# The attention branch's projection by one level of Strassen's method

## The chip, the cores and the metric

One Trainium2 chip, of which the kernel uses one core. The metric is the device time of one execution in microseconds. The kernel before takes 1419.27 us, the median of three runs (1418.53 to 1420.07). The engines are called PE (matrix multiply), ACT (activations, casts, copies), DVE (elementwise work), POOL, and SP, whose queue issues nearly every DMA.

## What is computed

One layer of an encoder on 1024 tokens of 1024 channels, in float32. The part that matters here is the end of the token mixer: two branches, attention `y_a` and recurrence `y_b`, each of 512 channels, are projected to 1024 channels, weighed by sigmoid gates, added, and projected once more.

```
p_a = y_a @ w_pa                      # (1024, 512) @ (512, 1024)
p_b = y_b @ w_pb
merged = sigmoid(gate_a) * p_a + sigmoid(gate_b) * p_b
mix = merged @ w_o
x = layer_norm(ALPHA * x + mix, ln1_g, ln1_b)
x = layer_norm(ALPHA * x + swiglu_ffn(x, w_ff_in, w_ff_out), ln2_g, ln2_b)
```

## The kernel before

**Precision.** PE multiplies in a rounded form of float32. Each operand is split into a high part (a cast on ACT) and a low part (a subtraction on DVE; `split`, line 444), and each product of two 128-row blocks is three matmuls: high by high, high by low, low by high (`mm3`, line 473). A matmul here takes a 128 x 128 weight block and 512 tokens, and accumulates in one of eight PSUM banks.

**Order of the work.** The program text does not run as written. `Plan` records every instruction with what it depends on; a list scheduler with a table of costs (`schedule`, line 183, repeated by `improve`, line 355) then sets one fixed order for each engine, and `issue` (line 387) emits it. So every row of the profile carries line 387, and rows are told apart by the names of tiles. Each engine works through its own order and waits where an operand or a buffer is not ready. Buffers come from pools by tag: six of `qk`, four each of `kb`, `pf`, `ph`, `tt`, two of `hl`, one each of `wr0` and `wr1` (raw weights), and so on. `plan.behind` makes the loads that follow it wait for a named earlier instruction.

**The stages around the change.** (1) The gate projections already use one level of Strassen's method, in pairs of output blocks (`GatePair`, line 1133, tiles `gs`, `Tgp`, `gu`, `gp`); their results go to DRAM (`gate_d`). (2) The loop at line 1273 projects the two branches, attention first (`i == 0`, from `ya_d`), then recurrence (`i == 1`, from `yb_d`). For each of four 128-channel chunks it loads the tokens (`yr`; the attention branch as two partial sums that DVE adds) and splits them into `yh` and `yl`. For each of eight output blocks `fb` and each half `hf` of the tokens it runs 4 chunks x 3 matmuls into one bank (tile `pps`), loads the stored gate (`sg`, tag `ph`), takes its sigmoid on ACT, and multiplies. Attention writes the result into `mraw` (tiles `m`), recurrence adds to it and prepares the operands of the next stage (`merged`, line 1256). Branch by branch that is 8 x 2 x 12 = 192 matmuls. (3) The residual's tokens `z`, eight loads of 512 KB, are written after this loop (line 1310), and the scheduler puts them where buffers of tags `qk` and `hl` come free. (4) The output projection `w_o`, by Strassen's method as well (tiles `oa`, `ob`, `Top`, `ms`), adds to `z`; then comes the first layer norm with transposes (tile `x1t`), and the feed-forward part (tiles `fe`, `fa`, `fb`, `fc`, `p`).

The inner loop of stage 2, before:

```python
for fb in range(KC):
    mf = mraw[fb // 4][:, fb % 4, :]
    if fb % 2 == 0:
        wp = weights(a["w_p"][i, fb // 2], [2, 4, P], f"wp{i}_{fb}")
    hi, lo = wp[fb % 2]
    w = [(hi[:, c], lo[:, c]) for c in range(4)]
    for hf in range(2):
        sg = half("ph", f"sg{i}_{fb}_{hf}")
        sync.dma_start(sg, gate_d[i, fb, :, hs(hf)])
        act.activation(sg, sg, AF.Sigmoid)
        o = bank(CYC[nbank % 5], f"pps{i}_{fb}_{hf}")
        nbank += 1
        project(o, w, hf, 4, lambda c: (yh[c], yl[c]))
        if i == 0:
            dve.tensor_mul(mf[:, hs(hf)], o, sg)
```

Of the kernel before, what the change touches and what calls it, by code (L numbers as in the profile page):

```python
# [8 lines left out]
F32R = mybir.dt.float32r  # L9
BF16 = mybir.dt.bfloat16  # L10
U16 = mybir.dt.uint16
AF = mybir.ActivationFunctionType
# [4 lines left out]
P = 128  # L17
S = 1024
D = 1024
KC = D // P  # L20
NT = S // P
HA, DH = 8, 64
HB = 4
NB = 512
# [366 lines left out]
def trunk(ctx: ExitStack, tc, a: dict, out: bass.AP):  # L391
    nc = tc.nc
    plan = Plan(tc)
    sync, act, dve, pool, pe = (plan.queue(n, e) for n, e in (
        ("SP", nc.sync), ("ACT", nc.scalar), ("DVE", nc.vector), ("POOL", nc.gpsimd), ("PE", nc.tensor)))
# [178 lines left out]
    b12 = block(0, 1, ("qk", "qk"), "b12")  # L574
    b22 = block(1, 1, ("qk", "qk"), "b22")
# [15 lines left out]
    T1, T2, T4, T3 = rows(b12), rows(b22), rows(b21), rows(b11)  # L591
# [113 lines left out]
    b22 = block(1, 1, ("hl", "hl"), "b22_2")  # L705
# [14 lines left out]
    ya_d = dram.tile([4, 2, 2, DH, S], F32, name="ya_d")  # L720
# [163 lines left out]
    raw = half("gt", "once_r")  # L884
# [15 lines left out]
    yb_d = dram.tile([4, P, S], F32, name="yb_d")  # L900
# [179 lines left out]
    gate_d = dram.tile([2, KC, P, S], F32, name="gate_d")  # L1080
# [52 lines left out]
    class GatePair:  # L1133
# [83 lines left out]
    loaded = len(plan.calls) - 1  # L1217
# [31 lines left out]
    mraw = [take("v", [4, S], "m0"), take("m", [4, S], "m1")]  # L1249
# [23 lines left out]
    for i, src in enumerate((ya_d, yb_d)):  # L1273
        yh, yl = [], []
        for c in range(4):
            if i == 0:
                raw, rest = (take(f"wr{a_}", [S], f"yr{a_}{c}") for a_ in range(2))
                plan.behind = (loaded,)
                for a_, t in enumerate((raw, rest)):
                    for j in range(2):  # L1280
                        sync.dma_start(t[j * DH:(j + 1) * DH], src[c, j, a_])
                plan.behind = ()
                dve.tensor_add(raw, raw, rest)
            else:
                raw = raw_load(src[c], [S], f"yr{i}{c}")
# [7 lines left out]
            hi, lo = wp[fb % 2]  # L1293
            w = [(hi[:, c], lo[:, c]) for c in range(4)]
            for hf in range(2):
                sg = half("ph", f"sg{i}_{fb}_{hf}")
                sync.dma_start(sg, gate_d[i, fb, :, hs(hf)])
                act.activation(sg, sg, AF.Sigmoid)
# [3 lines left out]
                if i == 0:  # L1302
                    dve.tensor_mul(mf[:, hs(hf)], o, sg)
                else:
                    dve.tensor_mul(sg, o, sg)
                    dve.tensor_add(mf[:, hs(hf)], mf[:, hs(hf)], sg)
                    merged(fb % 4, fb // 4, hf)


    z = [full(UTAGS[i], f"z{i}") for i in range(8)]  # L1310
    REST = UTAGS[8:]
    for t in range(NT):
        sync.dma_start(z[t], a["x"][blk(t), :])

    lnst = keep([P, NT * 12 + 2 * KC], "lnst", F32, "mask")
    lncol = lnst[:, NT * 12:].rearrange("p (i c) -> p i c", i=2)
# [142 lines left out]
    w = wo_T("p1")  # L1459
# [3 lines left out]
    w = wo_T("p2")  # L1463
# [5 lines left out]
    w = wo_T("p5")  # L1469
# [3 lines left out]
    w, op = wo_T("p6"), from_raw("ms2", lambda c: mraw[1][:, c, hs(1)])  # L1473
# [3 lines left out]
    w, op = wo_T("p3"), from_raw("ms4", lambda c: mraw[1][:, c, hs(0)])  # L1477
# [5 lines left out]
    w, op = wo_T("p7"), from_raw("ms3", lambda c: mraw[0][:, c, hs(1)])  # L1483
# [8 lines left out]
    w = wo_T("p4")  # L1492
# [210 lines left out]
    for c in range(2, FC):  # L1703
        if c in (14, 17):
            hf = c // 17
# [40 lines left out]
    u = [half(("wh0", "wl0", "wh1", "wl1")[i], f"fu{i}") for i in range(4)]  # L1746
# [3 lines left out]
    for prod in ("p1", "p5", "p6", "p4", "p7", "p2"):  # L1750
# [3 lines left out]
        for g in range(len(GR)):  # L1754
            d, n = group(prod, ai[prod], g)
# [4 lines left out]
        for t in range(4):  # L1760
            o = acc[t]
# [29 lines left out]
    for t in range(4):  # L1791
# [117 lines left out]
```

## Time and profile before

| what | value |
|---|---|
| median of three runs | 1419.27 us |
| the profiled execution | 1421.05 us, of which the span on the core is 1419.3 us |
| PE, DVE, ACT busy over the span | 99%, 80%, 49% |
| matmuls | 6674 |
| attention branch's products on PE | from 602.9 to about 652 us |
| recurrence branch's products | to about 695.6 us |
| output projection, before the first transposes | to about 745.9 us |
| transposes of the first layer norm | to about 805.8 us |

The span counts from the first to the last instruction of the program; the 1.75 us between it and the profiled execution's own time lie outside the program's instructions. Matmuls are pipelined and their ends are modelled, so PE's busy share says little by itself: the distance from one matmul's start to the next is what tells whether PE waits. Busy times of DVE and ACT count an instruction from start to end, and the end of one overlaps the start of the next by some tens of ns, so the distance between starts is the price of one more instruction.

### The profile page before, as it was taken

To read this page: it belongs to the slowest core of one execution; us is meant where nothing else is said; L and a number is where in the kernel's file an instruction comes from. 1 tells how busy PE (TensorE), PEld (TensorE's weight loads), DVE (VectorE), ACT (ScalarE), POOL (GpSimd) and SP (SyncE) were. 2 spreads that over 40 slices of the span, in tenths; PEclk is the share of its full clock that TensorE was granted. 3 is DMA by queue.
4 is the path that set the end of the run, shared out by engine and by line. 5 is a ranking of instruction groups with operands and counts; after the bars stand their busy time and mean duration, and the time that the engine had idled before them with its cause. 6 is when DMAs were issued, how large, how long until landed. Compare 5 with 4: busy or idle time off the path is not lost.

```text
span 1419.3 us, 19099 instructions
## 1 busy us (share of the span) xinstructions
PE 1408.3 (99%) x6674; PEld 1169.2 (82%) x6674; DVE 1137.9 (80%) x1972; ACT 699.0 (49%) x1246; POOL 87.1 (6%) x108
## 2 busy tenths in 40 slices
PE   9999999999999999999999999999999999999997
PEld 7788888888888888888887788888888888888886
DVE  7995878899998977555998879876687976789597
ACT  5534589887687632243538942233323334434330
POOL 0000133420000000000001000000000000000001
PEclk9999999999999999999999999999999999999999
DMA  7448999811113686367433536533334336878632
GB/s 272 149 163 263 301 297 260 245 61 45 46 52 122 212 238 222 112 203 279 156 104 119 189 130 204 196 120 100 101 111 137 116 105 203 314 254 281 216 126 90
DMA packets 99504, 245.25 MB, mean 173 GB/s; under 512 B 11456, under 2 KB 12736, under 8 KB 99408
## 3 DMA queue, kind: packets, MB, share of 16 engines
q1 hardware_dynamic: 98256, 239.83, 51.5%
q0 software_dynamic: 1152, 4.19, 1.5%
q8 instruction: 53, 0.87, 0.2%
q14 instruction: 43, 0.35, 0.1%
HBM read 181.26 MB, written 62.72 MB: 172 GB/s over the span
## 4 chain that ended last, share of the span: by engine, by line
PE 79%; ACT 1%; DVE 0%; issue 0%; DVEq 0%
PE p L387 15%; PE fb L387 12%; PE fc L387 8%; PE gs L387 8%; PE bps L387 7%; PE pps L387 6%; PE fa L387 5%; PE fe L387 3%; PE oa L387 3%; PE ob L387 2%; PE ge L387 2%; PE lp L387 2%; PE op L387 1%; PE pv L387 1%; PE pt L387 1%; PE x1t L387 0%
## 5 line engine op out<-in xcount | busy, mean ns | idle before, releaser
L387 PE MATMUL p<-dp 128*128 128x512 f32 (+1 forms) x957 | 210.0, 382 | 0.0
L387 PEld LDWEIGHTS p<-dp 128*128 128x128 f32 x957 | 175.3, 188 | 34.8
L387 PE MATMUL fc<-xs,Tp 128*128 128x512 f32 x528 | 128.9, 389 | 0.0
L387 PE MATMUL fb<-xs,Tp 128*128 128x512 f32 x528 | 127.8, 389 | 0.0
L387 ACT CAST Tp<-t 128x512 fp32r<-128x512 f32 x88 | 54.3, 620 | 131.3 <-PE fb L387 69.4
L387 PEld LDWEIGHTS fc<-xs,Tp 128*128 128x128 f32 x528 | 99.0, 188 | 20.8 <-ACT Tp L387 0.3
L387 PEld LDWEIGHTS fb<-xs,Tp 128*128 128x128 f32 x528 | 99.1, 188 | 20.6
L387 DVE TENSOR_TENSOR Tp<-t,Tp 128x512 fp32r<-128x512 f32 x88 | 60.3, 689 | 31.9 <-ACT Tp L387 31.6
L387 PE MATMUL fa<-x,Tp 128*128 128x512 f32 x336 | 81.4, 389 | 0.0
L387 PE MATMUL bps<-xl,wb_h 128*128 128x512 f32 x192 | 77.1, 402 | 0.0
L387 PE MATMUL bps<-xh,wb_h 128*128 128x512 f32 x192 | 76.6, 401 | 0.0
L387 PE MATMUL bps<-xh,wb_l 128*128 128x512 f32 x192 | 76.2, 400 | 0.0
L387 PEld LDWEIGHTS fa<-x,Tp 128*128 128x128 f32 x336 | 63.1, 188 | 13.1
L387 ACT CAST dp<-dap 128x1024 fp32r<-128x1024 f32 (+1 forms) x42 | 41.1, 980 | 58.3 <-PE p L387 35.6
L387 POOL TENSOR_TENSOR norm<-norm,few 128x1 f32<-128x1 f32 x16 | 12.8, 799 | 910.2 <-DVE norm L387 910.2
L387 DVE TENSOR_TENSOR dp<-dap,dp 128x1024 fp32r<-128x1024 f32 (+1 forms) x42 | 47.5, 1132 | 22.4 <-ACT dp L387 19.7
L387 DVE TENSOR_TENSOR tl<-pt,th 128x512 fp32r<-128x512 f32 (+1 forms) x96 | 52.1, 552 | 8.9 <-PE pv L387 4.2
L387 PE MATMUL fb<-x,Tp 128*128 128x512 f32 x240 | 57.8, 389 | 0.0
L387 ACT CAST th<-pt 128x512 fp32r<-128x512 f32 (+1 forms) x96 | 45.4, 477 | 16.6 <-PE pt L387 9.9
L387 PEld LDWEIGHTS fb<-x,Tp 128*128 128x128 f32 x240 | 45.0, 188 | 9.4
L387 PE MATMUL pps<-yh,wp_h 128*128 128x512 f32 x128 | 49.8, 389 | 0.0
L387 PE MATMUL pps<-yl,wp_h 128*128 128x512 f32 x128 | 49.8, 389 | 0.0
(789 smaller groups left out, 3536.3 us busy)
## 6 DMA issues: line engine op xcount, KB each, us to landing
dbp<-in_w_fo SPq DMA_DIRECT2D x45, 512.0 KB, 5.1
dap<-a_d SPq DMA_DIRECT2D x35, 512.0 KB, 4.9
wu_r<-in_w_ff SPq DMA_DIRECT2D x22, 512.0 KB, 4.0
wg_r<-in_w_ff SPq DMA_DIRECT2D x22, 512.0 KB, 4.0
a_d<-ar SPq DMA_DIRECT2D x42, 256.0 KB, 2.7
wop_r<-in_w_o SPq DMA_DIRECT2D x18, 512.0 KB, 3.7
a_d<-as SPq DMA_DIRECT2D x33, 256.0 KB, 3.6
qk_d<-qk SPq DMA_DIRECT2D x32, 256.0 KB, 5.1
```

What stands on the lines that cost most here:

```text
L387: getattr(q.engine, method)(*args, **kw)
```

## The change

The attention branch's projection leaves the loop and gets code of its own; the recurrence branch keeps the loop. The 512 channels are two halves of two chunks, the tokens two halves of 512, and a pair of output blocks two halves of 128 channels. Seven products of half size (2 chunks x 3 matmuls each) take the place of eight. The operands made from tokens (`y11`, `y12`, `y22`, `ys1` to `ys4`) are summed and split once, as soon as a chunk has been loaded, which the scheduler places among the gate stage's work. For each of the four pairs, DVE also makes four sums of weight blocks (`tpa`, `tpb`) and four splits of weights (`wpa` to `wpd`); of the seven products, one bank (`oa`) takes four and one (`oc`) two, each after ACT or DVE has taken out what was there; three sums (`pu1`, `pv5`, `pu2`) and four products with gates follow on DVE. The eight loads of `z` are put behind an instruction of the recurrence branch's block 3 (`begun`).

```diff
+    def branch_raw(i, c):
+        if i:
+            return raw_load(yb_d[c], [S], f"yr{i}{c}")
+        raw = take(f"wr{c // 2}", [S], f"yr{c}")
+        rest = full("pf", f"ys{c}")
...
+        dve.tensor_add(raw, raw, rest)
+        return raw
...
+    for c in range(2):
+        ra, rb = branch_raw(0, c), branch_raw(0, c + 2)
+        split(Y11[0][:, c], Y11[1][:, c], ra[:, hs(0)])
+        split(Y12[0][:, c], Y12[1][:, c], rb[:, hs(0)])
+        split(Y22[0][:, c], Y22[1][:, c], rb[:, hs(1)])
+        y24[c] = t = take("pf", [2, NB], f"y24_{c}")
+        if c == 0:
+            y3 = take("pf", [2, NB], "y3")
+        dve.tensor_sub(y3[:, c], ra[:, hs(0)], ra[:, hs(1)])
+        dve.tensor_add(t[:, 1], ra[:, hs(1)], rb[:, hs(1)])
+        dve.tensor_sub(t[:, 0], t[:, 1], ra[:, hs(0)])
+        split(YS1[0][:, c], YS1[1][:, c], t[:, 1])
+        dve.tensor_sub(t[:, 1], rb[:, hs(0)], t[:, 0])
+    for c in range(2):
+        split(YS2[0][:, c], YS2[1][:, c], y24[c][:, 0])
+    split(*YS3, y3)
+    for c in range(2):
+        split(YS4[0][:, c], YS4[1][:, c], y24[c][:, 1])
...
+    BC = (("s", "h", "s"), ("s", "h", "s"))
+    for n in range(KC // 2):
+        raw = raw_load(a["w_p"][0, n], [2, 4, P], f"wp0_{n}", n % 2)
+        b11, b21, b12, b22 = raw[:, 0, :2], raw[:, 0, 2:], raw[:, 1, :2], raw[:, 1, 2:]
+        ta, tb = (take("tt", [4, P], f"tp{x}_{n}") for x in "ab")
+        T1, T2, T3, T4 = ta[:, :2], ta[:, 2:], tb[:, :2], tb[:, 2:]
+        wa = half_split(raw[:, 0], 0, f"wpa_{n}")
+        dve.tensor_sub(T1, b12, b11)
+        dve.tensor_sub(T2, b22, T1)
+        wb = half_split(ta, 1, f"wpb_{n}")
+        dve.tensor_sub(T3, b22, b12)
+        dve.tensor_sub(T4, b21, T2)
+        wc = half_split(tb, 0, f"wpc_{n}")
+        wd = half_split(b22, 1, f"wpd_{n}")
+        oa, ob, oc = (bank(t, f"pps0_{n}{x}") for t, x in zip(BC[n % 2], "abc"))
...
+        mul(oa, wa, 0, Y11, True)
+        act.copy(u, oa)
+        mul(ob, wa, 1, Y12, True)
+        dve.tensor_add(u, ob, u)
+        dve.tensor_mul(m[0][:, hs(0)], u, gated(0, 2 * n, 0))
+        mul(oc, wb, 0, YS1, True)
+        v5 = half("tt", f"pv5_{n}")
+        act.copy(v5, oc)
+        mul(oa, wb, 1, YS2, False)
+        act.copy(u2, oa)
+        mul(oa, wc, 0, YS3, False)
+        dve.tensor_add(v5, oa, v5)
+        dve.tensor_mul(m[1][:, hs(1)], v5, gated(0, 2 * n + 1, 1))
+        mul(oc, wd, 0, YS4, False)
+        dve.tensor_add(u2, oc, u2)
+        dve.tensor_mul(m[1][:, hs(0)], u2, gated(0, 2 * n + 1, 0))
+        mul(oa, wc, 1, Y22, False)
+        dve.tensor_mul(m[0][:, hs(1)], oa, gated(0, 2 * n, 1))
+
+    for i in (1,):
...
+            if fb == 3:
+                begun = len(plan.calls) - 1
...
+    plan.behind = (begun,)
     for t in range(NT):
         sync.dma_start(z[t], a["x"][blk(t), :])
+    plan.behind = ()
```

From the feed-forward part's third chunk on, each engine's order is the same in both kernels, and so is all that stands ahead of the attention branch's loads in the gate stage. Between these two points three places matter.

PE, before, at the border of two groups of the attention branch (`pps_1_1` is output block 1, second half of the tokens, `pps_2_0` block 2, first half; `wp_0_h` and `wp_0_l` are the high and low weights, `yh`, `yl` the tokens):

```order
L387 MATMUL pps_1_1_1446<-yh_1428,wp_0_l_1438 128x512
L387 MATMUL pps_1_1_1446<-yh_1432,wp_0_h_1437 128x512
L387 MATMUL pps_1_1_1446<-yl_1433,wp_0_h_1437 128x512
L387 MATMUL pps_1_1_1446<-yh_1432,wp_0_l_1438 128x512
L387 MATMUL pps_2_0_1453<-yh_1420,wp_2_h_1448 128x512
L387 MATMUL pps_2_0_1453<-yl_1421,wp_2_h_1448 128x512
```

PE, changed kernel, in the first pair (`pps_0a`, `pps_0b`, `pps_0c` are its three banks, `pps_1a` the next pair's first; `ys_1426` holds `ys2` and `ys3`, `ys_1427` holds `ys4`):

```order
L387 MATMUL pps_0c<-ys1h,wpb_0h 128x512
L387 MATMUL pps_0c<-ys1l,wpb_0h 128x512
L387 MATMUL pps_0c<-ys1h,wpb_0l 128x512
L387 MATMUL pps_0b<-y12h,wpa_0l 128x512
L387 MATMUL pps_1a<-y11h,wpa_1h 128x512
L387 MATMUL pps_1a<-y11l,wpa_1h 128x512
L387 MATMUL pps_0a<-ys_1426,wpc_0h 128x512 x2
L387 MATMUL pps_0a<-ys_1426,wpc_0l 128x512
L387 MATMUL pps_0a<-ys_1426,wpc_0h 128x512 x2
L387 MATMUL pps_0a<-ys_1426,wpc_0l 128x512
L387 MATMUL pps_0c<-ys_1427,wpd_0h 128x512 x2
L387 MATMUL pps_0c<-ys_1427,wpd_0l 128x512
```

Ahead of these rows stand three more like the first three, and ahead of those the six of the second product in `pps_0a` (with `wpb`). Before, twelve matmuls fill a bank and nothing comes back to it; now a product of six returns to a bank that has held another, with products of other banks, and of the next pair, between the two.

DVE, before, in the attention branch (`m` are the merged results, `sg` the gates, `wp_4_l` a low part of weights):

```order
L387 TENSOR_TENSOR m_1412<-pps_0_0_1440,sg_0_0_1439 128x512
L387 TENSOR_TENSOR wp_4_l_1462<-wp_4_r,wp_4_h_1461 128x512
L387 TENSOR_TENSOR m_1412<-pps_1_0_1444,sg_1_0_1443 128x512
L387 TENSOR_TENSOR m_1412<-pps_0_1_1442,sg_0_1_1441 128x512
L387 TENSOR_TENSOR m_1412<-pps_1_1_1446,sg_1_1_1445 128x512
L387 TENSOR_TENSOR wp_4_l_1464<-wp_4_r,wp_4_h_1463 128x512
```

DVE, changed kernel, the same place, the first pair's results:

```order
L387 TENSOR_TENSOR pu_0_1453<-pps_0b,pu_0_1453 128x512
L387 TENSOR_TENSOR wpa_1l<-wp_1_r,wpa_1h 128x512
L387 TENSOR_TENSOR m_1412<-pu_0_1453,sg_0_0_1455 128x512
L387 TENSOR_TENSOR pv_0_1456<-pps_0a,pv_0_1456 128x512
L387 TENSOR_TENSOR wpb_1l<-tpa_1461,wpb_1h 128x512
L387 TENSOR_TENSOR pu_0_1454<-pps_0c,pu_0_1454 128x512
L387 TENSOR_TENSOR tpb_1462<-wp_1_r 128x256
L387 TENSOR_TENSOR tpb_1462<-wp_1_r,tpa_1461 128x256
L387 TENSOR_TENSOR m_1412<-pv_0_1456,sg_1_1_1457 128x512
L387 TENSOR_TENSOR m_1412<-pu_0_1454,sg_1_0_1458 128x512
L387 TENSOR_TENSOR wpd_1l<-wp_1_r,wpd_1h 128x256
L387 TENSOR_TENSOR m_1412<-pps_0a,sg_0_1_1459 128x512
```

For the same four blocks of results DVE now has three sums more, and splits and sums of the next pair's weights among them.

SP, before, near the end of the attention branch (`z` are the residual's tokens, `sg_1_0` a gate of the recurrence branch, `wp_2_r` raw weights):

```order
L387 DMA wp_2_r<-in_w_p 128x1024
L387 DMA sg_0_0_1503<-gate_d 128x512
L387 DMA z_1554<-in_x 128x1024
L387 DMA sg_1_0_1507<-gate_d 128x512
L387 DMA z_1555<-in_x 128x1024
L387 DMA z_1556<-in_x 128x1024
```

SP, changed kernel, in the recurrence branch (`wop_1_r` is a load of the output projection's weights):

```order
L387 DMA sg_5_0_1571<-gate_d 128x512
L387 DMA wop_1_r<-in_w_o 128x1024
L387 DMA z_1591<-in_x 128x1024
L387 DMA sg_5_1_1573<-gate_d 128x512
L387 DMA z_1592<-in_x 128x1024
L387 DMA z_1593<-in_x 128x1024
L387 DMA z_1594<-in_x 128x1024
L387 DMA sg_6_0_1581<-gate_d 128x512
L387 DMA z_1595<-in_x 128x1024
```

Three more loads of `z` follow, and then the gates `sg_6_1` and `sg_7_0`. The loads moved from the start of the recurrence branch to the stretch ahead of its last five gates.

More of the change, by code (lines that the diff above doesn't have):

```diff
@@ L1272, in trunk @@
     nbank = 0
-    for i, src in enumerate((ya_d, yb_d)):
+    def branch_raw(i, c):
[3 more added lines that the diff above has]
+        rest = full("pf", f"ys{c}")
+        plan.behind = (loaded,)
+        for n, t in enumerate((raw, rest)):
+            for j in range(2):
+                sync.dma_start(t[j * DH:(j + 1) * DH], ya_d[c, j, n])
+        plan.behind = ()
+        dve.tensor_add(raw, raw, rest)
+        return raw
@@ new lines, in gated, with pair_op @@
+    def gated(i, fb, hf):
+        sg = half("ph", f"sg{i}_{fb}_{hf}")
+        sync.dma_start(sg, gate_d[i, fb, :, hs(hf)])
+        act.activation(sg, sg, AF.Sigmoid)
+        return sg
+    def pair_op(tags, name):
+        return [take(t, [2, NB], f"{name}{n}", F32R) for n, t in zip("hl", tags)]
+    Y11, Y12, Y22, YS1 = (pair_op(tags, n) for tags, n in ((("qk", "qk"), "y11"), (("qk", "qk"), "y12"),
+                                                          (("qk", "qk"), "y22"), (("hl", "hl"), "ys1")))
@@ new lines, in trunk @@
+    ys23 = take("x", [2, 2, 2, NB], "ys23", F32R)
+    YS2, YS3 = ([ys23[:, i, j] for j in range(2)] for i in range(2))
+    ys4 = take("x", [2, 2, NB], "ys4", F32R)
+    YS4 = [ys4[:, 0], ys4[:, 1]]
+    y24 = [None, None]
+    y3 = None
+    for c in range(2):
[11 more added lines that the diff above has]
+        dve.tensor_sub(t[:, 1], rb[:, hs(0)], t[:, 0])
@@ new lines, in trunk, with half_split, mul @@
+    for c in range(2):
[3 more added lines that the diff above has]
+        split(YS4[0][:, c], YS4[1][:, c], y24[c][:, 1])
+    def half_split(src, lane, name):
+        hi, lo = (take(f"w{x}{lane}", [4, P], f"{name}{x}", F32R) for x in "hl")
+        n = src.shape[1]
+        split(hi[:, :n], lo[:, :n], src)
+        return hi, lo
+    BC = (("s", "h", "s"), ("s", "h", "s"))
[13 more added lines that the diff above has]
+        oa, ob, oc = (bank(t, f"pps0_{n}{x}") for t, x in zip(BC[n % 2], "abc"))
+        def mul(o, w, k, op, first):
+            more = {} if first else {"skip_group_check": True}
+            for c in range(2):
+                mm3(o, w[0][:, 2 * k + c], w[1][:, 2 * k + c], op[0][:, c], op[1][:, c], first and c == 0, c == 1, more)
+        m = [mraw[(2 * n + j) // 4][:, (2 * n + j) % 4, :] for j in range(2)]
+        u, u2 = (half("gt", f"pu{x}_{n}") for x in "12")
+        mul(oa, wa, 0, Y11, True)
[16 more added lines that the diff above has]
+        dve.tensor_mul(m[0][:, hs(1)], oa, gated(0, 2 * n, 1))
@@ L1274, in trunk @@
+    for i in (1,):
         yh, yl = [], []
         for c in range(4):
[L1276 to L1285, printed above, removed]
+            raw = branch_raw(i, c)
@@ L1295, in trunk @@
             for hf in range(2):
-                sg = half("ph", f"sg{i}_{fb}_{hf}")
-                sync.dma_start(sg, gate_d[i, fb, :, hs(hf)])
-                act.activation(sg, sg, AF.Sigmoid)
+                sg = gated(i, fb, hf)
                 o = bank(CYC[nbank % 5], f"pps{i}_{fb}_{hf}")
```

10 lines of the change are left out of this document (4 added, 6 removed).

## The prediction

> **What bounds the kernel now.** I read the page's first lines, then PE's order of time in the stage that changes, then the busy times by stage, then what PE waited for.
>
> ```profile
> span 1419.3 us, 19099 instructions
> ...
> PE 1408.3 (99%) x6674; PEld 1169.2 (82%) x6674; DVE 1137.9 (80%) x1972; ACT 699.0 (49%) x1246; POOL 87.1 (6%) x108
> ```
>
> PE is the busiest engine, but its busy share rests on modelled ends, so I look at starts. These are PE's rows in the attention branch, the first and the last of 37 that follow each other:
>
> ```profile
> 614.67 0.39 PE L387 MATMUL pps<-yh,wp_h 128*128 128x512 f32 x1
> ...
> 622.83 0.39 PE L387 MATMUL pps<-yh,wp_h 128*128 128x512 f32 x1
> ```
>
> 36 steps in 8.16 us are 0.2267 us from start to start, with no larger step among them. The stages around, each with microseconds, then busy time (and count) of PE, PEld, DVE, ACT and POOL, the granted clock and the DMA share:
>
> ```profile
> 520.00:548.00 28.00, 28.00 (x125) 23.20 (x124) 26.53 (x41) 8.85 (x13) 0.00 (x0) 1.00 0.78 230
> 602.90:652.10 49.20, 49.20 (x219) 40.76 (x218) 24.49 (x34) 22.48 (x34) 0.00 (x0) 1.00 0.64 208
> 652.10:695.60 43.50, 43.50 (x194) 36.03 (x193) 33.41 (x52) 19.90 (x33) 0.00 (x0) 1.00 0.66 237
> 695.60:745.90 50.30, 50.30 (x223) 41.67 (x222) 48.14 (x74) 19.52 (x27) 1.05 (x2) 1.00 0.35 115
> 745.90:805.80 59.90, 58.31 (x282) 45.25 (x280) 48.63 (x90) 54.60 (x110) 3.93 (x7) 1.00 0.46 148
> ```
>
> The rows are a piece of the gate stage, the attention branch, the recurrence branch, the output projection, and the first layer norm with its transposes. In the first four PE has no gap: 125 matmuls in 28.00 us are the same pace. The clock is granted in full. Only the last has a gap, 59.90 - 58.31 = 1.59 us. PE's own waits from 740 to 812 us name what ended them (total, times, longest); from 500 to 746 us the same view has no row.
>
> ```profile
> PE x1t L387 <- ACT r L387: 0.8, 2, 0.6
> PE oa L387 <- ACT Top4h L387: 0.6, 1, 0.6
> ```
>
> So PE bounds the changed stage: a matmul fewer there is 0.2267 us less, as long as the other engines still deliver in time.
>
> **What the change removes.** All matmuls of both branches' projections, and the multiplications by gates that close the attention branch's groups:
>
> ```profile
> L387 PE MATMUL pps<-yh,wp_h x128: 389/389/389, 603.1 to 694.9; 128*128 128x512 f32 x128
> L387 PE MATMUL pps<-yl,wp_h x128: 389/389/389, 603.3 to 695.1; 128*128 128x512 f32 x128
> L387 PE MATMUL pps<-yh,wp_l x128: 389/389/389, 603.6 to 695.4; 128*128 128x512 f32 x128
> ...
> L387 DVE TENSOR_TENSOR m<-pps,sg x16: 687/692/692, 611.5 to 652.3; 128x512 f32<-128x512 f32 x16
> ```
>
> 384 matmuls in two branches are 192 in one. Afterwards there are 4 pairs x 7 products x 2 chunks x 3 = 168 of the same shape. 24 fewer at 0.2267 us: **-5.44 us**.
>
> The Trainium skill ("TensorE: Matmul & The Clock Gate", section "Back-to-back issue gap") gives about 131 ns per matmul of 512 columns for a sustained stream in a real kernel and about 216 ns for an isolated one. By the first, 24 matmuls would be worth an estimated 3.1 us, by the second 5.2 us; this trace does not agree with the first, since its stream steps by 227 ns.
>
> **What it adds on DVE, and what hides it.** The price of one more DVE instruction is the step between starts:
>
> ```profile
> 520.32 1.22 DVE L387 TENSOR_TENSOR yl<-yr,yh 128x1024 fp32r<-128x1024 f32 x1
> 521.45 1.28 DVE L387 TENSOR_TENSOR gp<-gs,gp 128x512 f32<-128x512 f32 x2
> 522.77 0.69 DVE L387 TENSOR_TENSOR gu<-gs,gp 128x512 f32<-128x512 f32 x1
> 523.38 0.68 DVE L387 TENSOR_TENSOR tg<-wg_r 128x512 f32<-128x512 f32 x1
> ...
> L387 DVE TENSOR_TENSOR tl<-pt,th 128x256 fp32r<-128x256 f32 x16 | 6.7, 419 | 1.8 <-PE pv L387 1.8
> ```
>
> That is 1.13 us for 1024 columns (521.45 - 520.32) and 0.60 for 512 (523.38 - 522.77 is 0.61, and two in 1.28 less 0.68 are 0.60). For 256 columns I take the duration less the same overlap of 0.08: 0.34.
>
> In the changed order, from the last gate pair's first sum to the attention branch's last result, DVE has 52 instructions of 512 columns, 14 of 256 and 5 of 1024: 31.2 + 4.8 + 5.7 = 41.7 us. The old order has 33 of 512 and 4 of 1024 between the same two, 24.3 us, which the row 602.90:652.10 confirms with 24.49. PE's time for the stretch falls from 49.20 to 43.8 us. So DVE is busy 41.7 of 43.8 us, 95%, where it was half idle. Does that still hide? The row 520.00:548.00 has DVE at 26.53 of 28.00, also 95%, with PE without a gap, and the row 695.60:745.90 has 96% and again none. Both are built like the new stage: sums, splits and evictions between products. I also followed the new order by hand. The tightest place is the third pair's first product: after the second pair's last matmul in `pps_1b`, PE has 14 matmuls, 3.2 us, until it wants the low part of `wpa_2`. DVE first does a sum, a multiplication and that split, 1.8 us, and starts some 0.2 us after the matmul. That leaves 1.1 us. I take **0**; the bounds come with the rivals.
>
> At the branch's end DVE is later against PE than before. It still has its last few instructions to do when PE begins the recurrence branch, by the hand count 3.2 us of them against 0.9 us before (the last `m<-pps,sg` starts at 652.3 us and takes 0.69). The extra 2.3 us fits into the recurrence branch, where DVE is busy 33.41 of 43.50 us. I take 0, and keep +2.3 us as a bound.
>
> In the gate stage, DVE gets 16 instructions of 512 columns and six of 256 for four of 1024: 7.1 us more, spread over the stage. The densest piece (28.00 us above) has only 1.47 us free; there the new order holds about 2 us more. Bound 0 to +2.0, taken 0, since PE's operands there are made several products ahead.
>
> **What it adds on ACT.** Three copies out of a bank per pair and more, smaller casts. Their prices:
>
> ```profile
> L387 ACT COPY ge<-ge 128x512 f32<-128x512 f32 x12 | 7.0, 586 | 9.6 <-PE ge L387 5.9 <-issue 3.6
> L387 ACT COPY gp<-gs 128x512 f32<-128x512 f32 x2 | 1.2, 589 | 0.0
> ```
>
> Twelve copies at 0.59 us are 7 us, on an engine that was busy 22.48 of 49.20. Between the second and the third product in `pps_0a` stand nine matmuls, 2.04 us, for one copy of 0.59: hidden, 0.
>
> **What it moves.** The eight loads of `z` go from 650 us to behind the second load of the output projection's weights. The queue's rows before, then the first reader of `z`, and how long its loads took to land:
>
> ```profile
> 649.99 0.33 SPq L387 DMA_DIRECT2D z<-in_x  x1
> ...
> 676.39 0.33 SPq L387 DMA_DIRECT2D wop_r<-in_w_o  x1
> 676.96 10.86 SPq L387 DMA_DIRECT2D sg<-gate_d  x5
> ...
> L387 DVE SCALAR_TENSOR_TENSOR z<-z,oa x4: 679/680/680, 706.2 to 710.0; 128x512 f32<-128x512 f32 x4
> ...
> DMA to landing us min/median/max: 5.4/7.6/10.3
> ```
>
> In the new order they are issued at about 676.4 - 5.4 = 671 us and land, at up to 10.3 us each and overlapped, by about 685; their first reader moves from 706.2 to 700.8. So `z` itself is in time. Queued behind them are the gates `sg_6_1`, `sg_7_0` and `sg_7_1` and the next weights. I take 0 and treat a late gate as a rival.
>
> **Sum.** The profiled execution's 1421.05 - 5.44 = 1415.6 us. The median of the runs lies 1.78 us below that execution (1419.27), so the forecast is **1413.8 us**. What comes behind is not made anew: from the feed-forward part's third chunk on the order is the same, so the shift carries to the end. In the layer norm the order is shuffled, with the same 64 transposes. Its gap of 1.59 us may go or be tripled: -1.6 to +3.2 us, taken 0.
>
> **Rivals.** *Waits at reused banks (slower).* Each pair now returns to `oa` three times and to `oc` once, 16 times in all, and PE must not come back before ACT or DVE has emptied the bank. If the two cannot follow (it decides when DVE's step exceeds its slack, 41.7 us growing beyond 43.8, so that evictions queue), PE waits each time. The only such waits in the trace are 0.4 us on average and 0.6 at most (the rows of `x1t` and `oa` above): 16 x 0.6 = 9.6 us, less 5.44, is +4.2 us: 1423.4 us. Below 0.34 us each it stays faster. Against it: the gate stage reuses banks in the same way, and PE's waits there have no row. 5%.
>
> The Trainium skill ("Perfetto Trace Analysis", section "Matmuls") says independent matmul groups should rotate through different banks so that emptying one overlaps the next group's matmuls. By it, bank reuse speaks against this change and for this rival. The trace does not bear that out where products of other banks stand between, as in the gate stage.
>
> *DVE late into the output projection.* The 2.3 us are not made good, because DVE is 96% busy there: 1416.1 us. 10%.
>
> *A late gate.* `sg_6_1` is issued behind the eight loads of `z`. The gate loads' times from issue to landing before:
>
> ```profile
> DMA to landing us min/median/max: 2.6/3.6/9.4
> ```
>
> Issued at about 676 us, the slowest, 9.4 us, would land at 685.4, and the sigmoid takes 0.6; its product is ready at about 685. One microsecond: 1414.8 us. 7%.
>
> *The gain is given back.* ACT is busy 54.60 of 59.90 us in the layer norm, more than PE's matmuls need; if its work there does not start earlier, the saved time becomes a longer gap: 1419.3 us. Against it: ACT's work there follows PE's products, which all come earlier. 6%.
>
> **How the numbers follow.** Forecast 72%, the others as named. Low: 1413.8 less the 1.6 us of the gap and 0.4 us for half the runs' spread on one side, 1411.8. High: 1413.8 + 3.2 = 1417.0, which also takes in the late DVE and the late gate. What is left out is the given-back gain and the slower case, 11%, and a little of the tails. About 0.2%, 2.8 us, is what a measurement of this kernel tells from no change, so faster means below 1416.4: 72 + 7 + 7 of the late DVE's 10 = 86%. Within: 6 + 3 = 9%. Slower: 5%.
>
> **What would show it.** In the changed profile, PE's starts in the attention branch still step by 0.227 us, the recurrence branch's first matmul starts about 5.4 us earlier, and so do the first `oa` and the first feed-forward product `p`. DVE is busy about 95% from 603 to 647 us with PE's waits empty. Rows of PE waiting for `pu`, `pv` or `wp` would show the first rival; DVE idle before a gate with a DMA behind it, the third; a larger gap between 740 and 805 us, the fourth. I am wrong if DVE's work on operands cannot be laid beside the products at 95%, or if the shuffled layer norm costs more than 3 us.

## The result and the profile after

The changed kernel takes 1412.18 us (median of 4 runs, 1412.10 to 1414.53) against 1419.67 us for the kernel before on the same chip (1418.53 to 1420.97): a ratio of 0.9951, with a 95% interval of 0.9934 to 0.9968. The forecast was 1413.8 us, faster, with a range of 1411.8 to 1417.0. The profiled execution of the changed kernel took 1412.10 us. Its first lines:

```profile
span 1410.3 us, 19118 instructions
...
PE 1399.7 (99%) x6650; PEld 1162.8 (82%) x6650; DVE 1161.6 (82%) x2025; ACT 710.5 (50%) x1275; POOL 87.3 (6%) x108
```

24 matmuls fewer, and 23.7 us more of VectorE's work (1137.9 before). (In the rows PE is TensorE, DVE is VectorE and ACT is ScalarE.) The busy times by stage, in the columns of the prediction (microseconds; busy time and count of PE, PEld, DVE, ACT, POOL; granted clock; DMA share): a piece of the gate stage, the attention branch, the recurrence branch, the output projection, the first layer norm.

```profile
520.00:548.00 28.00, 27.95 (x124) 22.86 (x123) 26.45 (x43) 8.39 (x15) 0.00 (x0) 1.00 0.74 230
601.00:645.00 44.00, 44.00 (x196) 36.44 (x195) 34.68 (x61) 27.43 (x48) 0.00 (x0) 1.00 0.59 191
645.00:688.00 43.00, 43.00 (x192) 35.59 (x191) 37.65 (x59) 22.77 (x37) 0.00 (x0) 1.00 0.78 281
688.00:738.30 50.30, 50.30 (x224) 41.59 (x223) 46.38 (x68) 20.08 (x28) 0.93 (x1) 1.00 0.37 116
738.30:796.00 57.70, 57.01 (x278) 45.00 (x277) 47.71 (x91) 53.12 (x106) 4.58 (x7) 1.00 0.45 151
```

PE still has no gap in either branch, and the pace is the same: 196 matmuls in 44.00 us are 4.45 per microsecond, as were the 219 in 49.20 of before. In the layer norm the gap has shrunk from 1.59 to 57.70 - 57.01 = 0.69 us. Of PE's waits from 500 to 812 us one row is left; the two waits for `r` are gone:

```profile
PE oa L387 <- ACT Top4h L387: 0.6, 1, 0.6
```

Where the time went, from the starts of the same matmuls in both traces (us; the first gate matmul writes `gs`, the last matmul of the recurrence branch is the last `pps`, `ob` is the start of the output projection's product p3, `fa` the feed-forward part's third chunk):

| stretch | before | after | difference |
|---|---|---|---|
| start to the 101st matmul | 28.61 | 26.58 | -2.03 |
| 101st matmul to first `gs` | 451.91 | 451.89 | -0.02 |
| first `gs` to last `pps` | 214.84 | 209.71 | -5.13 |
| last `pps` to first `ob` of p3 | 39.67 | 39.67 | 0.00 |
| first `ob` of p3 to first `fa` | 194.64 | 192.91 | -1.73 |
| first `fa` to the end | 489.61 | 489.56 | -0.05 |

Three stretches differ, and only the middle one is the change itself. The first lies 500 us ahead of it, in a piece whose order of matmuls is the same. Windows at the start, of before and then of after:

```profile
4.00:8.00 4.00, 3.72 (x8) 2.30 (x8) 3.04 (x8) 1.99 (x5) 0.00 (x0) 1.00 0.87 274
8.00:12.00 4.00, 4.00 (x14) 3.15 (x14) 2.94 (x6) 2.75 (x5) 0.00 (x0) 1.00 1.00 370
```

```profile
4.00:8.00 4.00, 3.15 (x13) 2.10 (x13) 3.16 (x8) 2.00 (x5) 0.00 (x0) 1.00 0.92 301
8.00:12.00 4.00, 4.00 (x19) 3.33 (x18) 2.87 (x6) 2.69 (x6) 0.00 (x0) 1.00 1.00 369
```

In the profiled execution of before matmuls still start 0.43 us apart until about 9.8 us; in that of after they reach 0.23 us at 7 us. It differs from execution to execution of one kernel: below, a run that shares the changed kernel's order up to 595 us reaches its 101st matmul at 28.77 us and not at 26.58. (The granted clock reads 1.00 in all four rows; that PE runs at half speed there is read from the steps.) So the profiled spans differ by 8.95 us, of which 2 are this accident, while the medians differ by 7.5.

### The profile page after: what moved, and what is told of

It reads as the page before. It is cut to its first block, busy times and chain, and to the rows that moved or that the text cites. A ratio compares the mean times of both kernels' runs of the same rounds, so it can differ in the third digit from the quotient of the medians.

```text
span 1410.3 us, 19118 instructions
## 1 busy us (share of the span) xinstructions
PE 1399.7 (99%) x6650; PEld 1162.8 (82%) x6650; DVE 1161.6 (82%) x2025; ACT 710.5 (50%) x1275; POOL 87.3 (6%) x108
## 4 chain that ended last, share of the span: by engine, by line
PE 79%; DVE 1%; issue 0%; DVEq 0%
PE p L387 15%; PE fb L387 12%; PE gs L387 9%; PE fc L387 8%; PE bps L387 7%; PE fa L387 5%; PE fe L387 3%; PE pps L387 3%; PE oa L387 3%; PE ob L387 2%; PE ge L387 2%; PE lp L387 2%; PE op L387 1%; PE pv L387 1%; PE pt L387 1%; PE x1t L387 0%
## 5 line engine op out<-in xcount | busy, mean ns | idle before, releaser
L387 DVE TENSOR_TENSOR u<-fb,p 128x512 f32<-128x512 f32 x40 | 27.6, 690 | 22.7 <-PE fb L387 22.5
L387 PEld LDWEIGHTS bps<-xl,wb_h 128*128 128x128 f32 x192 | 36.2, 189 | 6.3
```

Of the source, the lines that this page charges most:

```text
L387: getattr(q.engine, method)(*args, **kw)
```

## Experiments

Every edit makes the planner lay out the whole program anew. Eight of the twelve runs therefore keep the planner's order on every engine and drop, add or move instructions only when they are issued. The hook, the same in all of them:

```
-            for _, i in order:
+            for i in self.kept(order):
...
                 getattr(q.engine, method)(*args, **kw)
+                for m_, a_, k_ in self.extra.get(i, ()):
+                    getattr(q.engine, m_)(*a_, **k_)
+
+    def kept(self, order):
+        seq = [i for _, i in order if i not in self.skip and i not in self.hold]
```

**24 matmuls left out of the kernel before.**

```
                 project(o, w, hf, 4, lambda c: (yh[c], yl[c]))
+                if i == 0:
+                    plan.skip.update(base + 3 * c + 2 for c in range(1, 3 - hf))
```

> The kernel before, its order of instructions kept on every engine, with 24 matmuls of the attention branch left out (the low part of the weights times the high part of the values, for two of four chunks in the first half of tokens and one of four in the second; the output lacks these small terms). Nothing is added on VectorE or ScalarE. Theory (TensorE sets the pace at 0.2267 us per matmul): the last matmul of the recurrence branch comes 5.44 us earlier, counted from the first matmul of the gate stage so that differences at the program's start drop out, and the end follows: 1414.2 us against 1419.7. Since the order is kept, the layer norm's gap stays near 1.6 us, so this kernel stays about 1.7 us behind the changed one. Rival (131 ns per matmul, the figure of the Trainium skill, TensorE: Matmul & The Clock Gate, section Back-to-back issue gap): an estimated 3.1 us, 1416.5 us. Rival (the gain is given back in the layer norm because ScalarE does not start earlier): the branch's end 5.4 us earlier, but the first feed-forward product p hardly at all.

Measured: 1413.79 us against 1419.39 of before, ratio 0.9961 [0.9947, 0.9975]. From the first `gs` to the last `pps` 209.40 us against 214.84: **-5.44 us, to the hundredth** what 24 x 0.2267 gives. The 131 ns of the Trainium skill ("TensorE: Matmul & The Clock Gate", section "Back-to-back issue gap"; an estimated 3.1 us) do not hold for this stream. The rival that the layer norm gives the gain back seemed at first to have a part in it: in the profiled execution 1.50 of the 5.44 us are lost there (196.15 us from first `ob` of p3 to first `fa`, before 194.64), though the order and PE's waits are those of before. The windows around the place, of this run and, 5.6 us later, of before, show why:

```profile
758.40:761.20 2.80, 1.98 (x9) 1.12 (x9) 2.80 (x4) 2.50 (x6) 0.00 (x0) 0.97 0.00 0
761.20:764.40 3.20, 3.20 (x10) 2.51 (x10) 3.15 (x6) 2.83 (x6) 0.00 (x0) 0.50 0.00 0
```

```profile
764.00:766.80 2.80, 1.97 (x9) 1.13 (x10) 2.80 (x4) 2.51 (x6) 0.00 (x0) 1.00 0.00 0
766.80:770.00 3.20, 3.20 (x17) 2.59 (x17) 3.20 (x7) 3.14 (x8) 0.00 (x0) 1.00 0.00 0
```

The column third from the end is the granted clock. After the same stretch, in which PE is busy 2.0 of 2.8 us, the clock fell to 0.50 for 3.2 us in one execution and not in the other: 10 matmuls in the time of 17. It is an accident of the execution and not of the edit, as far as the runs tell: three other profiled executions with this order in the layer norm do not have it, and this one, which also has the late start, took 1416.91 us, where the four others took 1413.4 to 1413.9.

**24 matmuls added to the changed kernel.**

```
+                if c == 0 and op is not Y22:
+                    plan.extra[len(plan.calls) - 1] = [("matmul", (o, w[1][:, 2 * k], op[1][:, 0]),
+                                                        {"start": False, "stop": False, **more})]
```

> The changed kernel, its order of instructions kept on every engine, with 24 matmuls added: in the first chunk of six of each pair's seven products the low part of the weights times the low part of the operand goes into the same bank. As many matmuls as before the change, with the change's work on VectorE and ScalarE and its loads. Theory: all of the branch's gain was matmuls, so 5.44 us come back between the first matmul of the gate stage and the first of the output projection, 1417.6 us, and only the layer norm's 1.7 us and what lies at the start remain of the gain. Rival (VectorE, not TensorE, sets the pace of the new branch): the added matmuls lie beside VectorE's work and cost clearly less than 5.4 us, below 3.

Measured: 1417.89 us, ratio to before 0.9990 [0.9980, 0.9999]; 5.71 us more than the changed kernel by the medians, 215.30 - 209.71 = 5.59 us from first `gs` to last `pps`. So PE and not VectorE sets the new branch's pace, and with as many matmuls as before only some 1.5 us of the gain are left. They are in the layer norm: 192.89 us there, as in the changed kernel.

**The loads of z pushed back, nothing else (kernel before).**

```
+            at = seq.index(self.until) + 1
+            seq[at:at] = [i for _, i in order if i in self.hold]
...
         sync.dma_start(z[t], a["x"][blk(t), :])
+        plan.hold.add(len(plan.calls) - 1)
```

> The kernel before, its order kept on every engine, with only the eight loads of z moved on the queue: behind the second load of the output projection's weights, as in the change. Theory: 0.0 us at every landmark, 1419.7 us, since z lands before its first reader. Rival (a late gate behind the eight loads): 1.0 us or more later at the end of the recurrence branch. Rival (the moved loads are what shortened the layer norm's gap): the layer norm 1.7 us shorter, 1418 us.

Measured: 1425.61 us, 6.2 us slower, ratio 1.0044 [1.0029, 1.0059]. My theory of 0.0 failed. The rival of a late gate came true, at more than the 1.0 us that I had named as its least size. The queue's rows (issue; the eight loads are 512 KB each), then PE's waits from 480 to 830 us that are not in before:

```profile
677.00 0.33 SPq L387 DMA_DIRECT2D wop_r<-in_w_o  x1
677.74 5.41 SPq L387 DMA_DIRECT2D z<-in_x  x8
683.25 13.08 SPq L387 DMA_DIRECT2D sg<-gate_d  x5
```

```profile
PE pps L387 <- DVE sg L387: 3.3, 1, 3.3
PE oa L387 <- DVE sg L387: 1.3, 1, 1.3
```

Five gates stand behind all eight loads, ScalarE waits 9.4 us for one of them, and PE stops twice, which costs 3.63 us (89.08 - 85.45, last `gs` to last `pps`) in the branches and 1.6 us in the output projection. (The last microsecond lies in other stages: 0.75 us ahead of the gates, 0.34 behind the first `fa`.) The layer norm takes 194.63 us as before, so the rival that moved loads shorten it fails.

**The changed kernel without the wait on z.**

```
-    plan.behind = (begun,)
     for t in range(NT):
         sync.dma_start(z[t], a["x"][blk(t), :])
```

> The changed kernel without the wait on the loads of z; the order is planned anew. Theory: the attention branch keeps its 168 matmuls and its 5.4 us; what is planned anew afterwards may move the layer norm by -1.6 to +3.2 us against the kernel before: 1411.5 to 1417. Rival (the moved loads are needed for the gain, because the early loads hold up gates or weights in the new branch): VectorE or ScalarE waits for a DMA in the attention or recurrence branch, TensorE has waits there, and less than 4 us of the 5.4 are left at the first matmul of the output projection.

Measured: 1423.54 us, ratio to before 1.0029 [1.0017, 1.0041]: 11.4 us slower than the changed kernel. The theory failed and the rival is right, though what comes late are tokens and neither gates nor weights. The plan is new, but up to 640 us PE has no stall that the changed kernel has not. The queue's rows, the last value of the recurrence branch on ScalarE, and PE around its longest wait:

```profile
639.88 1.08 SPq L387 DMA_DIRECT2D yr_r<-yb_d  x1
641.05 0.38 SPq L387 DMA_DIRECT2D z<-in_x  x1
...
642.14 1.11 SPq L387 DMA_DIRECT2D z<-in_x  x2
...
645.53 1.61 SPq L387 DMA_DIRECT2D z<-in_x  x2
...
650.05 0.33 SPq L387 DMA_DIRECT2D yr_r<-yb_d  x1
```

```profile
658.41 1.04 ACT L387 CAST yh<-yr_r 128x1024 fp32r<-128x1024 f32 x1 [0.54 <-DMA yr_r<-yb_d]
```

```profile
654.48 0.39 PE L387 MATMUL pps<-yh,wp_l 128*128 128x512 f32 x1
659.51 2.07 PE L387 MATMUL pps<-yh,wp_h 128*128 128x512 f32 x4 [4.64 <-ACT yh L387]
661.38 1.48 PE L387 MATMUL pps<-yl,wp_h 128*128 128x512 f32 x3
```

The planner put the loads of `z` from 634 to 647 us, and the last of the four loads of the recurrence branch's values, `yr`, comes behind them: it is issued at 650.05 us and lands 8.3 us later, where in the changed kernel it is issued at 640.37 us and none takes more than 4.8. The kernel before, whose planner had no such wait either, issues its last `yr` ahead of all loads of `z`, which begin at 649.99 us:

```profile
638.11 0.32 SPq L387 DMA_DIRECT2D yr_r<-yb_d  x1
```

In the changed kernel the last `yh` is made at 645.39 us:

```profile
645.39 1.05 ACT L387 CAST yh<-yr_r 128x1024 fp32r<-128x1024 f32 x1
```

PE waits 4.6 us for it and 1.0 us for an earlier `yh`, and runs at about half clock behind the long wait (661.38 - 659.51 is 1.87 us for four matmuls; the granted clock was 0.53 from 659.51 to 663.00 us). From first `gs` to last `pps` it takes 217.91 us, 8.20 more than the changed kernel and 3.07 more than before. **Planned without the wait, the Strassen step is a loss in this plan**, in its own stages already. The layer norm of this plan costs another 2.6 us. No run has the Strassen step with the loads of `z` where they stood before, behind all loads of `yr`, and this is one draw of the planner, so the run shows what these loads cost ahead of `yr` and not that the step needs them as late as the changed kernel has them.

**Work added on VectorE (changed kernel).** The subtraction that makes each low part is repeated once, twice or three times; in a fourth run only one subtraction per pair is repeated, once.

```
         split(hi[:, :n], lo[:, :n], src)
+        plan.extra[len(plan.calls) - 1] = [("tensor_sub", (lo[:, :n], src, f(hi[:, :n])), {})] * 1
```

> The changed kernel, its order kept on every engine; each of the 16 subtractions that make a low part of the branch's weights (12 of 512 columns, 4 of 256) is done a second time, right behind the first, to the same result: 12 x 0.60 + 4 x 0.34 = 8.6 us more of VectorE's work in the attention branch. In the changed kernel VectorE is idle about 10 us between 601 and 650 us of its trace, 6.3 of them before the second pair and 3.7 in the three pairs behind. Theory (work is free until VectorE's idle time in the pairs is used up): the three later pairs get 6.4 us against 3.7 idle, and the rest is made good in the recurrence branch, where 5.35 of 43 us are free: 0 to +1 us, 1412.2 to 1413.2. Rival (a late low part stops TensorE at once, slack or not): up to +8.6 us. Rival (VectorE never matters here): 0.0 at this dose and at the next two.

> As the run with one repetition, with two: 17.2 us more of VectorE's work. Theory: about 9 us more than the idle time of the three later pairs, of which some 5 are made good in the recurrence branch: +3 to +5 us, about 1416, and TensorE's waits name the low parts of the weights or the sums behind the banks. This is the point at which the slower rival of the prediction begins. Rival (VectorE never matters here): 0.

> As before, with three repetitions: 25.8 us more. Theory: VectorE now sets the pace of the branch, so this dose costs its whole 8.6 us on top of the run with two: +11 to +14 us against the changed kernel, 1423 to 1426, slower than the kernel before. Rival (VectorE never matters here): 0.

> The changed kernel, its order kept, with one subtraction per pair done a second time, the one that makes the low part of the second operand (4 x 0.60 = 2.4 us more of VectorE's work; 1.8 of it in the three later pairs, where VectorE is idle 3.7 us). Theory (a threshold: up to about 3.5 us of additional work the branch does not notice): 0 to +0.5 us, 1412.2 to 1412.7. Rival (no threshold; the runs with one, two and three repetitions cost 5.2, 13.1 and 22.2 us, about 0.6 to 0.9 us per added microsecond): +1.4 to +2.1 us, 1413.6 to 1414.3.

| more work on VectorE | median, us | ratio to before, 95% | first `gs` to last `pps` | more than changed |
|---|---|---|---|---|
| 2.4 us | 1413.53 | 0.9961 [0.9946, 0.9975] | 210.33 | +0.62 |
| 8.6 us | 1417.35 | 0.9985 [0.9975, 0.9994] | 214.02 | +4.31 |
| 17.2 us | 1425.25 | 1.0040 [1.0025, 1.0055] | 222.49 | +12.78 |
| 25.8 us | 1434.35 | 1.0105 [1.0088, 1.0122] | 232.07 | +22.36 |

PE's waits from 490 to 850 us with one repetition, and with three:

```profile
PE pps_2a L387 <- DVE wpa_2l L389: 2.1, 1, 2.1
PE pps_3a L387 <- DVE wpa_3l L389: 0.8, 1, 0.8
PE oa L387 <- ACT Top4h L387: 0.6, 1, 0.6
PE pps_2c L387 <- DVE pu L387: 0.2, 1, 0.2
...
```

```profile
PE pps_2a L387 <- DVE wpa_2l L389: 5.2, 1, 5.2
PE pps_3a L387 <- DVE wpa_3l L389: 4.4, 1, 4.4
PE pps_1a L387 <- DVE wpc_1l L389: 1.7, 1, 1.7
PE pps_1c L387 <- DVE pu L387: 1.5, 1, 1.5
...
```

Some 4 us of the three larger doses are free (8.6 less 4.31, 17.2 less 12.78, 25.8 less 22.36 are 4.3, 4.4 and 3.4); the 3.7 us of idle time in the three later pairs come close. It is no sharp threshold, since 2.4 us already cost 0.62. My theory put the threshold at 9 us and missed all three sizes (0 to 1, 3 to 5 and 11 to 14 us), because I let the rest be made good in the recurrence branch. That was the mistake: VectorE has idle time there, PE has none, and what PE has lost once it never gains back.

With two and three repetitions a part of the loss is TensorE's clock: behind the two longest waits the granted clock was 0.50 and 0.52 (633.5 to 636.4 and 646.6 to 649.8 us) with two, and 0.50 (636.4 to 641.0 and 653.0 to 657.5 us) with three. With one repetition, whose longest wait is 2.1 us, it stayed at 1.00.

The run with 2.4 us is unclear by its total (1.35 us over the changed kernel's median, between the two forecasts, and its trace has lost 1.1 us between the 101st matmul and the first `gs`, far ahead of the branch); in the stage itself it costs 0.62 us, a little over the theory and far from 1.4.

As for what stops PE, the low parts of the weights cost most and the reused banks (`pu`) less, but the smallest dose stops it at such a bank: the first matmul in `pps_2c` starts 0.48 us after the one ahead of it instead of 0.23, the largest step in that run's branch.

**The wait on z alone, planned anew (kernel before).**

```
+    plan.behind = (begun,)
     for t in range(NT):
         sync.dma_start(z[t], a["x"][blk(t), :])
+    plan.behind = ()
```

> The kernel before with only the wait for the loads of z added (they follow the fourth group of the recurrence branch, as in the change), the order planned anew. Theory: the planner, which now knows of the wait, puts the gates of the recurrence branch between or ahead of the loads, unlike the run that only pushed the eight loads back; so the 5 us of waits for gates are gone and the branches take what they took before: 1419.4 us, with -1.6 to +3.2 us from the layer norm's order. Rival (the late loads of z cost a gate in the old branches whatever the order): +4 to +6 us, about 1425.

Measured: 1425.75 us, ratio 1.0046 [1.0031, 1.0061], as the rival said, but not for its reason. From last `gs` to last `pps` it takes 85.45 us, exactly as before, so the moved loads cost the branches nothing. The time goes earlier, in stages that the edit does not touch: 520.57 us from the 401st matmul to the last `gs` against 513.12, where this plan's longest wait is

```profile
PE pv L387 <- ACT th L387: 3.8, 1, 3.8
```

So the theory's total (1422.6 us at most) failed, while what it said of the branches holds. Why this plan loses the rest there stays open.

**z where the change has it, order of before kept.** One load, a gate, three loads, a gate, four loads:

```
+            for mark, part in zip((self.until, *self.marks), (zs[:1], zs[1:4], zs[4:])):
+                at = seq.index(mark) + 1
+                seq[at:at] = part
```

> The kernel before, its order kept on every engine, with only the loads of z moved on the queue to where the changed kernel has them: one behind the second load of the output projection's weights, three behind the next gate, four behind the gate after that. Theory (the run that moved all eight together lost 4.6 us because five gates stood behind them; two gates between them are enough): 0 to +0.5 us at the first matmul of the output projection, 1419.4 to 1419.9 us. Rival (it is the volume of the late loads, not their place among the gates, that delays the gates): again 2 to 5 us late there, 1422 to 1425. Rival (the moved loads bring the gain in the layer norm): 1.7 us faster, 1417.7.

Measured: 1420.73 us against 1418.96, ratio 1.0010 [1.0001, 1.0020]. Both branches take what they took (214.84 us from first `gs` to last `pps`), and the first matmul of the output projection comes as early as before, as the theory had it; within that first product PE then waits once:

```profile
PE oa L387 <- DVE sg L387: 0.9, 1, 0.9
```

From the last `pps` to p3 it costs 1.19 us (40.86 against 39.67). So the place among the gates makes most of the difference (5.2 us lost with all eight together, 1.2 with gates between them), and it does not quite cover everything: the median is 1.8 us up, over the theory's 0 to 0.5. The layer norm is that of before (194.61 us): the moved loads do not shorten it. The changed kernel has the same eight loads among its gates,

```profile
668.85 0.33 SPq L387 DMA_DIRECT2D z<-in_x  x1
669.28 0.38 SPq L387 DMA_DIRECT2D sg<-gate_d  x1
669.76 1.34 SPq L387 DMA_DIRECT2D z<-in_x  x3
671.19 0.63 SPq L387 DMA_DIRECT2D sg<-gate_d  x1
671.91 2.80 SPq L387 DMA_DIRECT2D z<-in_x  x4
675.90 1.96 SPq L387 DMA_DIRECT2D sg<-gate_d  x2
```

and no such wait.

**Another draw of the planner's search, for both kernels.**

```
-        vary = np.random.default_rng(1)
+        vary = np.random.default_rng(2)
```

> The changed kernel, planned with another draw of the search's random numbers; the same instructions in another order. Theory: the plan moves the total by several us either way (the re-planned runs showed +6.5 from a wait ahead of the gate stage and 2.6 us of spread in the layer norm), while the attention and recurrence branches keep their 360 matmuls at 0.227 us: 81.6 us from the first matmul of the attention branch to the last of the recurrence branch, as far as gate products do not stand between. Total 1409 to 1420. Rival (the new branch is so tight on VectorE that another order opens waits in it): PE's waits name the sums, the low parts or the banks of the branch, 1 us or more.

> The kernel before, planned with the same other draw. Theory: without the change the branches hold 384 matmuls, 87.0 us, with no waits in them; total 1415 to 1427, and the changed kernel with this draw is faster than it by 5.4 us, give or take the 3 us by which plans differ elsewhere. Rival (the gain is luck of one plan): no difference, or the other sign.

Measured: 1415.04 us (ratio to before 0.9970 [0.9958, 0.9982]) with the change and 1425.58 us (1.0050 [1.0032, 1.0068], 1422.8 to 1430.4) without. From last `gs` to last `pps` 79.79 and 85.45 us, the same as with the first draw, and no waits there. (5.66 us are 25 matmuls: one more of the branch's first stands ahead of the last `gs` in the changed order. From the first `gs` it is 216.10 and 212.05 us, which says nothing of the change: in these plans the first `gs` stands at another place, with 971 and 947 matmuls from there to the last `pps` in place of 935 and 959.) The branches' gain belongs to the change; how much lies around it belongs to the plan (the two kernels differ by 10.5 us with this draw and by 7.5 with the first). In the layer norm (first `ob` of p3 to first `fa`) six executions with the changed kernel's order lie between 192.89 and 192.92 us; before's order gives 194.61 to 194.65 in three executions and 196.15 in the one at half clock; the other plans give 193.84, 193.99, 194.36 and 195.53.

## Why the prediction was right, and where it was not

**The matmuls (-5.44 us): right.** Both runs that change only their number give it, 5.44 without VectorE's work and 5.59 with it.

**VectorE's work is hidden: right, but the share was wrong, and so was the tightest place.** I set 41.7 us of work against PE's 43.8 us, 95%. The row of 601 to 645 us has 34.68 of 44.00, 79%. The 41.7 us, from the last gate pair's first sum to the branch's last result, lay between about 596 and 650 us; I had measured the stretch on PE, whose branch begins later and ends earlier. But the share does not decide; single places do. The prediction walked one by hand: 1.1 us of margin at the low part of `wpa_2`. Its row on VectorE, and the matmul that reads it:

```profile
623.31 0.69 DVE L387 TENSOR_TENSOR wpa_2l<-wp_r,wpa_2h 128x512 fp32r<-128x512 f32 x1
```

```profile
624.95 0.39 PE L387 MATMUL pps_2a<-y11h,wpa_2l 128*128 128x512 f32 x1
```

624.95 less 624.00 is 0.95 us, close to the hand count, and one repetition of all low parts stopped PE longest at this place. It is not the tightest one. The run with 2.4 us of added work stopped PE at a bank instead, and there the changed kernel has less room. VectorE has emptied `pps_1c` at 624.85 + 0.68 = 625.53 us, and the next pair's first matmul in `pps_2c` starts at 626.08: 0.55 us. (That PE waits there for this `pu` is shown by the row `pps_2c <- DVE pu` of the run with one repetition.)

```profile
624.85 0.68 DVE L387 TENSOR_TENSOR pu<-pps_1c,pu 128x512 f32<-128x512 f32 x1
```

**The gate stage (0 to +2.0, taken 0): +0.31.** That is the difference between -5.44 and the -5.13 of the table; 0.21 of it at one place in the densest piece, where PE steps 0.44 us instead of 0.23:

```profile
529.89 0.39 PE L387 MATMUL gs<-xl,Tgp_4h 128*128 128x512 f32 x1
530.33 0.70 PE L387 MATMUL gs<-gs,Tgp_4h 128*128 128x512 f32 x2
```

**The moved loads (taken 0, a late gate 1 us): right for the changed kernel, and misjudged as a part.** In their present place they cost nothing there, and in the old order 1.2 us in the output projection's first product, close to the rival's price. What the prediction did not see is what the wait is for. It asked what is queued behind `z` in the new place, and not what the planner would queue behind it without the wait: the last values of the next branch. In the one plan without it, the branches took 8.2 us longer than in the changed kernel.

**The layer norm (-1.6 to +3.2, taken 0): -1.73**, just outside the lower bound, and a property of the plan. 0.90 us of it are PE's gap, which shrank from 1.59 to 0.69; the other 0.8 us are not explained. It is why the time came out below the forecast: 1419.27 - 5.44 + 0.31 - 1.73 = 1412.4, measured 1412.18. That the time stayed within the range, by 0.4 us, is luck in this term: the prediction allowed for a smaller gap and gave no reason to expect one. The 1.78 us that the profiled execution of before lay above its median are about the 2 us of its late start; that this is their cause is not shown.

**The rivals.** Reused banks: no wait at them in the changed kernel; with work added they stop PE as well, at the smallest dose before anything else in the branch, but the weights' low parts cost more. (Of the two rows from which the prediction took 0.6 us as a price, `x1t` is a wait for a bank; `oa` waits for an operand, `Top4h`.) The rival's turning point was right in kind, VectorE's step beyond its slack. Its size, 43.8 less 41.7 or 2.1 us, was too small: some 4 us of added work were free, with 8.6 us more the kernel is still 2 us faster than before, and with 17.2 it is slower. VectorE late into the output projection: its last result was done 4.9 us after the start of the branch's last matmul (I said 3.2 us of work; 1.3 of the 4.9 are a wait for a gate's sigmoid) and delayed nothing, 0.00 in the table. The gain given back in the layer norm: no.

## What to carry to other kernels

Where one engine works without a gap, count what its instructions cost from start to start and take that as the gain; then look for the one operand or the one bank that is ready last, not for the other engine's share. Time that the bound engine loses is not made good by slack on the other engines later. A large load that is moved must be asked about at both places: what waits behind it at the new one, and what would wait behind it at the earlier one. And where a planner redoes the order, keep the order by hand in experiments; a re-planned kernel lost 7.4 us in stages that its edit did not touch.

## What the runs showed of the hardware

In one execution TensorE's clock fell to half without a long wait. In the run with 24 matmuls left out it was at full speed, then fell to 0.50 for 3.2 us after a stretch in which PE was busy 1.98 of 2.80 us, which cost 1.5 us; in before, behind the same stretch, it stayed at 1.00. The Trainium skill ("TensorE: Matmul & The Clock Gate", section "What's actually happening") says that the clock is set by a free-running window of about 3.4 us, halved after an idle one and full after a busy one. The 3.2 us and the dependence on the execution agree with that; that the window must be idle does not, since here PE was more than half busy and its longest gap was 0.60 us.
